# Two decoder layers on one core: the convolution's b gate by seven products instead of eight, its token sums in parts, and where its weights are summed and split

## The chip, the core and the metric

The kernel runs on one core of a Trainium2 chip. A core has five engines that run beside each other and wait for each other by semaphores: TensorE (PE in the profile; its weight loads are listed as PEld), VectorE (DVE), ScalarE (ACT), GpSimd (POOL) and SyncE (SP), which issues most of the DMAs. Operands lie in SBUF, 128 partitions wide; TensorE writes its sums to PSUM, eight banks of 128 x 512 numbers of 32 bits. The metric is the device time of one execution in microseconds, as the median of several runs; less is better. The profile is of one execution, taken by the hardware profiler.

## The reference

x has 512 tokens of 1024 features. Two layers: the first mixes tokens by attention with forget gates (16 heads), the second by a short gated convolution. Each is followed by an MLP with squared ReLU and by gated input embeddings, and all of them have norms before and behind. The part that the change is about is the second layer's mixer:

```python
def short_conv(h, w_in, conv_w, w_out):
    D = h.shape[-1]
    proj = h @ w_in
    b_gate = proj[..., :D]
    c_gate = proj[..., D:2 * D]
    u = proj[..., 2 * D:]
    z = c_gate * u
    zc = lax.conv_general_dilated(z, conv_w[:, None, :].astype(z.dtype), ...)
    return (b_gate * zc) @ w_out
```

and around it, for every layer,

```python
    x = x + rmsnorm(m, g[1])
    f = sq_relu_mlp(rmsnorm(x, g[2]), w_mlp_up[i], w_mlp_down[i])
    x = x + rmsnorm(f, g[3])
    gate = jax.nn.sigmoid(rmsnorm(x, g[4]) @ w_ple_gate[i])
    e = (p[i] @ w_ple_proj[i]) * gate
    x = x + rmsnorm(e, g[5])
```

## The kernel before

**Number format.** Every 32-bit operand of a matmul is split in a high part, rounded to the format that TensorE takes (a cast on ScalarE, L299), and a low part, the rest (a subtraction on VectorE or GpSimd, L300; the helper is `split`). A product is then three matmuls, high by high (L291), high by low and low by high (L292, L293; the helper is `mm3`). So each tile of weights, 128 x 512, costs a load of 256 KB, a cast and a subtraction before TensorE can use it. Casts and subtractions of tokens go by the same two lines.

**Weights.** `plan` lists all weight tiles in the order of use. `wide(key)` gives one of them and, first, has the next ones up to SOON = 8 beyond it loaded and split (`prepare`). Loads go through 14 raw buffers on SP's queue, split tiles through pages: there are 70 pages of 128 x 512, shared by nearly everything that lives in SBUF.

**Order.** The program is written in the order of the computation, and a scheduler puts the instructions of each engine in order from it, by its own estimate of times. Some work is put off until a number of columns was streamed (`put_off`), or until `need` asks for it: the transposes of normed tokens for example (`pre_norm`, `rate`).

**Seven products.** Where a matrix product is cut in 2 x 2 blocks, seven block products and some sums give what eight do. The down projections of the MLPs work so (`down`), and in the convolution the products for c and u. There, token halves L and R (256 tokens each) and halves of the input features cut the tokens in four parts, a11 to a22; halves of input and output features cut the weights in four quarters, b11 to b22. Sums of token parts are s1 to s4, sums of weight quarters t1 to t4. A unit, named 0, 2, 4 or 6 after the first of its two feature tiles, has seven products (`product`), each of two weight tiles and of 24 matmuls with 256 columns: four feature slices, three matmuls each, once for c and once for u. The results stay in PSUM until VectorE has combined them after COMBINE (L913; product 1 is copied by ScalarE first). `end` multiplies c by u (L925), and `finish` applies the three taps (L836 on ScalarE, L839 on VectorE), multiplies by b (L843) and splits the result, y.

**b.** b is a plain product, `times_b`: for each of eight feature tiles eight slices of three matmuls, with 512 columns; for unit 0 in two token halves (bL, bR). Its weights are 16 tiles, wcb.

**Order of the convolution.** CONV_ORDER lists, by unit, the products' numbers and the other steps: "embed" (a part of layer 1's embeddings that TensorE does here), "sums" (`token_sums`: all of s1 to s4 and their splits, L865 and L299/L300), b, and "end". Tokens 256 to 511 are first needed after "embed", where `need` asks for their transposes.

**Weight sums.** t1 to t4 are made in DRAM, before the convolution, by DMAs on GpSimd's queue: a copy of one quarter (L211) and a DMA that adds another (L213), 4 units by 4 sums, 32 steps of 512 KB. `sum_weights` issues the next step; it is called twice for each of four token blocks in attention's output product and in the gate products of layer 0, and 18 times in layer 0's MLP.

**Around it.** The gate stage (`ple`) of layer 0 goes through eight blocks of tokens and halves of features; for each 128 tokens `residual` adds its result to x and `pre_norm` scales x to the convolution's normed tokens, into pages of its own (n0b_h), which TensorE transposes later (n0b_p, L354). ScalarE copies the transposed tokens too (hp, L1229), for the token sums. After the convolution `mixer_out` multiplies y by w_o of the convolution (co) in the order of BLOCKS, eight slices k for each block. In attention, `bias` loads the mask and decay of a head by four DMAs on SP (L596) and masks them on GpSimd (L597); `scores` reads them on VectorE (L616).

Of the kernel before, what the change touches and what calls it, by code (L numbers as in the profile page):

```python
# [26 lines left out]
LAG = 2  # L27
AHEAD = 2
# [28 lines left out]

QUARTERS = ("b11", "b12", "b21", "b22")
SUMS_W = {"t1": ("b11", "b12"), "t3": ("b12", "b22"), "t2": ("t1", "b22"), "t4": ("t2", "b21")}
SUM_STEPS = (  # L60
    ("t1", "copy"), ("t3", "copy"), ("t1", "add"), ("t3", "add"), ("t2", "copy"), ("t2", "add"),
    ("t4", "copy"), ("t4", "add"),
)
# [26 lines left out]
def trunk(ctx: ExitStack, tc, g4T, x, xT, pT, g, g0T, wv, wqk, bf, wo, wcs, wcb, cw, wco, wup, wdn, wpp, wpg, out):  # L90
# [28 lines left out]
    g4_cols = []  # L119
# [78 lines left out]
    sums_w = {n: dram.tile([4, P, 2 * S], F32, tag=f"ws{n}", name=f"ws{n}") for n in SUMS_W}  # L198

    sum_steps = [(name, kind, i) for name, kind in SUM_STEPS for i in range(4)]  # L200

    def sum_weights():

        if not sum_steps:
            return
        of = lambda n, i: sums_w[n][i] if n in sums_w else wcs[QUARTERS.index(n), i]
        name, kind, i = sum_steps.pop(0)
        a, b = SUMS_W[name]
        with tc.issue_after(behind["add"].ins):
            if kind == "copy":  # L210
                nc.gpsimd.dma_start(sums_w[name][i], of(a, i))  # L211
            else:
                nc.gpsimd.dma_start(  # L213
                    sums_w[name][i], of(b, i), accum_op=ALU.add, max_dma_last_dim=2048
                )
# [12 lines left out]
    for l in range(2):  # L228
        if l == 0:
            for c, (_, width) in enumerate(V_CHUNKS):  # L230
                for k in range(KT * width // 512 if width < 272 else KT):
                    plan(("v", c, k), wv[c][k])
            for i in range(KT):
                for j in range(4):
                    plan(("qk", i, j), wqk[i, j])
            plan_embed(0)
            for k in range(KT):
                for n in range(2):
                    plan(("o", n, k), wo[n, k])
        else:  # L240
            for i0, i in CONV_ORDER:
                if i == "embed":
                    plan_embed(1)
                elif i == "bL" or i == "b":
                    for j in range(4):
                        plan(("b", i0, j), wcb[i0 // 2, j])
                elif i in PARTS:
                    n = PARTS[i][1]
                    src = sums_w[n] if n in sums_w else wcs[QUARTERS.index(n)]
                    for s in range(2):  # L250
                        plan(("sq", i0, s, n), src[i0 // 2][:, s * S : (s + 1) * S])
            for n in range(2):
                for k in range(KT):
                    plan(("co", n, k), wco[n, k])
# [88 lines left out]
    def scaled(t, n, xs, r, gB, name):  # L343
        h = page(f"{name}_h{t}_{n}")
# [4 lines left out]
        return h  # L349
# [30 lines left out]
    def pre_norm(t, xs, gB, hT, name, also=None):  # L380

        r = stats(t, xs, name)
        hs = [scaled(t, n, xs, r, gB, name) for n in range(2)]
# [56 lines left out]
    def mixer_out(kind, lhs, xs, gB, then, opened):  # L440


        mgs, sums = {}, {}
        for t, n in BLOCKS:
# [3 lines left out]
            ps = opened.pop((t, n)) if at else bank(f"{kind}{n}_{t}")  # L448
            for k in range(KT - 1 if at else 0, KT):
                mm3(ps, lhs(k, t), wide(kind, n, k, soon=soon(t, n)), k == 0, k == KT - 1)  # L450
            sums[t, n] = squares(ps, f"{kind}s{n}_{t}")
            mgs[t, n] = gained(ps, gB, n, f"{kind}m{n}_{t}")
            if (t, 1 - n) in mgs:
# [5 lines left out]
                if kind == "o":  # L459
                    sum_weights()  # L460
# [14 lines left out]
    def attention(hT, first_xT, g0_col, first_x, by_hand):  # L475
# [108 lines left out]
        def bias(h):  # L584
# [9 lines left out]
            for b, pr in enumerate(probs[h]):  # L594
                n = (b + 1) * P
                nc.sync.dma_start(pr, neg_c[b, h : h + 1, :n].partition_broadcast(P))  # L596
# [197 lines left out]
        for c in range(-SCORED, n_sc + LAG):  # L794
# [21 lines left out]
        return oT[0], banks_o  # L816

    def conv(hT, plain):
        taps = consts.tile([P, KT, 3], F32, tag="taps", name="taps")
        nc.sync.dma_start(taps, cw)  # L820
        ys = []
# [12 lines left out]
        def finish(i, z, y, b):  # L834
# [8 lines left out]
            nc.vector.tensor_tensor(out=a[:, :S], in0=b, in1=a[:, :S], op=ALU.mult)  # L843
# [9 lines left out]
        def token_sums():  # L853

            kept_at = {}
            for j in range(2):
                p = {(c, n): plain[2 * c + j, n][:, :S] for c in range(2) for n in range(2)}
                for name, a, b, op in (
                    ("s3", p[0, 0], p[1, 0], ALU.subtract), ("s1", p[1, 1], p[1, 0], ALU.subtract),
                    ("s2", p[0, 0], "s1", ALU.add), ("s4", "s2", p[0, 1], ALU.subtract),  # L860
                ):
                    t = page(f"{name}_{j}")
                    a, b = (kept_at[u, j] if isinstance(u, str) else u for u in (a, b))
                    kept_at[name, j] = t[:, :S]
                    nc.vector.tensor_tensor(out=t[:, :S], in0=a, in1=b, op=op)  # L865
            four = lambda u: u.rearrange("p (k c) -> p k c", k=4)
            two = lambda u: u[:, :S].rearrange("p (k c) -> p k c", k=2)
            for name in ("s3", "s1", "s2", "s4"):
                A[name] = [
                    Pair(page(f"{name}h{d}", F32R), page(f"{name}l{d}", F32R)).at(two)  # L870
                    for d in range(2)
                ]
                for d in range(2):
                    for j in range(2):
                        at = slice(j * P, (j + 1) * P)
                        split(
                            A[name][d].hi[:, :, at], A[name][d].lo[:, :, at],
                            four(kept_at[name, j])[:, 2 * d : 2 * d + 2, :],
                        )
# [37 lines left out]

        def end(i0):

            have = got.pop(i0)  # L920
            for e in range(2):
# [4 lines left out]
                y = Pair(page(f"yh{i}", F32R), page(f"yl{i}", F32R))  # L926
                finish(i, z, y, banks_b.pop((i0, e)))
                ys.append(y)

        need(0, 1)  # L930
        for i0, i in CONV_ORDER:
            if i == "embed":
                need(*range(NB))
            if i == "sums":
                token_sums()
# [146 lines left out]
    def ple(l, hT, xs, rs, gB, then):  # L1082
# [100 lines left out]
    for l in range(2):  # L1183
# [38 lines left out]
        if l == 0:  # L1222
# [8 lines left out]
            def then(t):  # L1231
                pre_norm(t, xs[t], g0, hT, "n0b", copied)
# [14 lines left out]
def layout(x, p, norm_g, w_attn_in, b_forget, w_attn_out, w_conv_in, conv_w, w_conv_out,  # L1247
# [26 lines left out]
    got["wcb"] = tiles(b.reshape(D, D), 2, 256)  # L1274
    cu = np.stack([c, u]).reshape(2, 2, 4, P, 4, 2, P)
    got["wcs"] = cu.transpose(1, 5, 4, 3, 0, 2, 6)[[0, 0, 1, 1], [0, 1, 0, 1]].reshape(4, 4, P, 2 * S)
# [26 lines left out]
```

## Time and profile before

| | us |
|---|---|
| median of 3 runs | 1215.29 |
| lowest and highest run | 1214.1, 1215.66 |
| the profiled execution | 1215.53 |
| its span, first to last instruction | 1213.8 |

The page of the profile lists each engine's busy time, then the chain of work that ended last: followed back from the last instruction, at each step to what released it. An engine with a large share of that chain sets the time. The page's groups join instructions of one line, engine and operation: "wl<-raw,wh ... x82 | 52.2, 683" is 82 instructions that write wl, together 52.2 us busy, 683 ns each. The rows of a timeline are: start, duration, engine, line, operation, tiles, count. Matmuls are pipelined, so one's duration overlaps the next one's; the distance of their starts is what one costs in a stream. A row of waits is: who waited for whom, total us, times, longest.

### The profile page before, as it was taken

The numbers are of one execution on the slowest core, as the hardware profiler recorded it, in microseconds if no ns is written. First come the engines' busy times: TensorE is split into PE (matmuls) and PEld (weight loads), VectorE is DVE, ScalarE is ACT, GpSimd is POOL, SyncE is SP. The second block draws the span as 40 slices with busy tenths as digits, with TensorE's granted clock in tenths as the row PEclk, the third lists the DMA queues.
The fourth block names the chain that finished last, engine by engine and source line by source line (L and its number), as shares of the span: only waits on it lengthen the run. The fifth ranks groups of instructions, "written<-read, shape, count | busy, mean of one in ns | idle before, by whom it ended". The sixth has DMA issues, their size and how long they took to land.

```text
span 1213.8 us, 18739 instructions
## 1 busy us (share of the span) xinstructions
PE 1203.1 (99%) x6176; PEld 1028.0 (85%) x6176; DVE 910.2 (75%) x1389; ACT 697.8 (57%) x1435; POOL 662.3 (55%) x691
## 2 busy tenths in 40 slices
PE   9999999999999999999999999999999999999997
PEld 8888888898888888888889999889888888888886
DVE  5668888575698779869867888665767886679963
ACT  7567888557634654465666555235755445535652
POOL 3057677167977798876221000017769777777420
PEclk9999999999999999999999999999999999999999
DMA  9564442673565566528357445732322442244501
GB/s 308 189 183 128 134 126 65 220 245 94 123 172 140 148 164 173 151 72 264 122 153 212 144 153 172 245 129 81 119 72 88 139 132 80 67 139 130 182 19 52
DMA packets 95377, 173.91 MB, mean 143 GB/s; under 512 B 11248, under 2 KB 18464, under 8 KB 95024
## 3 DMA queue, kind: packets, MB, share of 16 engines
q1 hardware_dynamic: 90272, 155.67, 40.1%
q0 software_dynamic: 4864, 16.78, 6.5%
q8 instruction: 49, 0.80, 0.3%
q14 instruction: 48, 0.39, 0.1%
q10 hardware_dynamic: 144, 0.26, 0.1%
HBM read 164.20 MB, written 25.25 MB: 156 GB/s over the span
## 4 chain that ended last, share of the span: by engine, by line
PE 96%; ACT 2%; DVE 1%; issue 1%; DVEq 0%; POOLq 0%; POOL 0%; ACTq 0%
PE up L293 10%; PE up L292 10%; PE up L291 10%; PE dn L293 9%; PE dn L291 8%; PE dn L292 8%; PE pg L293 2%; PE pg L291 2%; PE pg L292 2%; PE sq L293 2%; PE sq L292 2%; PE sq L291 2%; PE qk L291 2%; PE qk L292 2%; PE qk L293 2%; PE sc L610 1%
## 5 line engine op out<-in xcount | busy, mean ns | idle before, releaser
L300 DVE TENSOR_TENSOR wl<-raw,wh 128x512 fp32r<-128x512 f32 (+1 forms) x400 | 375.0, 980 | 41.7 <-ACT wh L299 37.6
L299 ACT CAST wh<-raw 128x512 fp32r<-128x512 f32 (+1 forms) x400 | 218.3, 619 | 12.4 <-DMA raw<-in_wv 3.7
L292 PE MATMUL up<-hTl,wh 128*128 128x512 f32 (+1 forms) x576 | 209.9, 366 | 0.0
L293 PE MATMUL up<-hTh,wl 128*128 128x512 f32 (+1 forms) x576 | 208.9, 365 | 0.0
L291 PE MATMUL up<-hTh,wh 128*128 128x512 f32 (+1 forms) x576 | 208.7, 366 | 0.0
L300 POOL TENSOR_TENSOR wl<-T,wh 128x512 fp32r<-128x512 f32 x112 | 157.2, 1434 | 25.4 <-ACT wh L299 24.1
L970 ACT ACTIVATE r<-up 128x512 f32<-128x512 f32 (+1 forms) x72 | 39.4, 548 | 197.3 <-PE up L293 197.3
L1018 DVE TENSOR_TENSOR acc<-dn,acc 128x512 f32<-128x512 f32 x168 | 107.8, 678 | 31.1 <-PE dn L293 31.0
L292 PEld LDWEIGHTS up<-hTl,wh 128*128 128x128 f32 x576 | 108.6, 189 | 17.5
L293 PEld LDWEIGHTS up<-hTh,wl 128*128 128x128 f32 x576 | 108.7, 189 | 17.4
L291 PEld LDWEIGHTS up<-hTh,wh 128*128 128x128 f32 x576 | 108.0, 189 | 17.6
L161 POOL TENSOR_TENSOR T<-raw,raw 128x512 f32<-128x512 f32 x56 | 85.8, 1544 | 59.7 <-DMA raw<-in_wdn 28.2
L161 POOL TENSOR_TENSOR T<-raw,T 128x512 f32<-128x512 f32 x56 | 89.0, 1589 | 2.2
L321 POOL TENSOR_SCALAR cor_r_v<-cos,cos 128x1 f32<-128x1 f32 x4 | 1.2, 302 | 155.5 <-ACT junk L337 155.5
L299 ACT CAST wh<-T 128x512 fp32r<-128x512 f32 x112 | 61.5, 617 | 10.4 <-POOL T L161 10.4
L300 DVE TENSOR_TENSOR A12l<-q,A12h 128x512 fp32r<-128x512 f32 x28 | 30.1, 1074 | 42.8 <-ACT A12h L299 42.8
L300 DVE TENSOR_TENSOR A11l<-q,A11h 128x256 fp32r<-128x256 f32 x28 | 26.1, 933 | 35.9 <-ACT A11h L299 35.9
L1025 POOL TENSOR_TENSOR acc<-acc,acc 128x512 f32<-128x512 f32 x28 | 47.1, 1714 | 10.0 <-DVE acc L1018 10.0
L299 ACT CAST S1h<-s 128x512 fp32r<-128x512 f32 x28 | 17.4, 621 | 60.8 <-POOL s L985 60.8
L293 PE MATMUL pg<-wh,hTl 128*128 128x512 f32 (+1 forms) x136 | 51.8, 381 | 0.0
L291 PE MATMUL pg<-wh,hTh 128*128 128x512 f32 (+1 forms) x136 | 51.6, 379 | 0.0
L292 PE MATMUL pg<-wl,hTh 128*128 128x512 f32 (+1 forms) x136 | 51.4, 378 | 0.0
(327 smaller groups left out, 3302.2 us busy)
## 6 DMA issues: line engine op xcount, KB each, us to landing
raw<-in_wup SPq DMA_DIRECT2D x128, 256.0 KB, 2.9
raw<-in_wdn SPq DMA_DIRECT2D x128, 256.0 KB, 2.8
wst<-in_wcs POOLq DMA_DIRECT2D x24, 512.0 KB, 6.7
raw<-in_wqk SPq DMA_DIRECT2D x32, 256.0 KB, 4.8
raw<-in_wpg SPq DMA_DIRECT2D x32, 256.0 KB, 3.2
raw<-wst SPq DMA_DIRECT2D x32, 256.0 KB, 3.6
raw<-in_wcs SPq DMA_DIRECT2D x24, 256.0 KB, 4.0
g<-in_g SPq DMA_DIRECT2D x18, 256.0 KB, 5.4
```

Source lines behind the costliest of these rows:

```text
L161: nc.gpsimd.tensor_tensor(out=B[name, p], in0=B[a, p], in1=B[b, p], op=ALU.subtract)
L291: nc.tensor.matmul(ps, a.hi, b.hi, start=start, stop=False)
L292: nc.tensor.matmul(ps, a.hi, b.lo, start=False, stop=False)
L293: nc.tensor.matmul(ps, a.lo, b.hi, start=False, stop=stop)
L299: nc.scalar.copy(hi, src)
L300: eng.tensor_tensor(out=lo, in0=src, in1=hi.bitcast(F32), op=ALU.subtract)
L321: nc.gpsimd.tensor_scalar(out=v, in0=parts[0], scalar1=parts[1], scalar2=EPS, op0=ALU.add, op1=ALU.add)
L610: nc.tensor.matmul(ps[:, :nm], at[:, b * P : n], to[:, :nm], start=s == 0, stop=s == 1)
L970: nc.scalar.activation(r[:, :n], ps[:, :n], AF.Relu)
L1018: nc.vector.tensor_tensor(out=a, in0=banks[s], in1=a, op=ALU.add)
L1025: nc.gpsimd.tensor_tensor(out=a, in0=a, in1=acc[i, s][:, :S], op=ALU.add)
```

## The change

- **b by seven products.** Two more units, "b0" and "b4", give b for feature tiles 0 to 3 and 4 to 7, by the same `product`: what were c and u are now two pairs of b's feature tiles. The four quarters of the weights, and t1 to t4, have six units instead of four; `times_b` isn't called any more. `end` of a unit of c and u stops after the taps, and `end` of b0 or b4 weighs four results, in token halves (`weigh`), and splits them.
- **Token sums in parts.** `token_sums` makes s1 and s2 (splitting s2), then s3, then the split of s1, then s4, as steps of their own between the products of units 0 and 2, whose order is interleaved.
- **Normed tokens.** `pre_norm` writes them to the pages that held the gated embeddings' products of the same tokens (`freed`), not to new ones.
- **Splits in the gate stage.** Before the gate products' last two blocks in layer 0 four weight tiles more are prepared, and eight more at the start of the convolution.
- **Weight sums.** The copies (24 now) go to SP's queue, two after each `bias` of heads 2 to 15; the additions (24) stay on GpSimd's, one at each block of attention's output product.
- **Output product of the convolution.** Slices k are taken in the order 0, 1, 2, 3, 4, 6, 5, 7, and the first four of them for two blocks ahead of the rest.

```diff
+CO_ORDER = (0, 1, 2, 3, 4, 6, 5, 7)
+CO_FIRST = 4
+SPLIT_AT = {"s1s2": "s2", "s3": "s3", "s1": "s1", "s4": "s4"}
+SUMS_OF = {"s1s2": ("s1", "s2"), "s3": ("s3",), "s1": (), "s4": ("s4",)}
+UNITS = (0, 2, "b0", 4, 6, "b4")
 CONV_ORDER = (
-    [(0, i) for i in (1, 2, "bL", "embed", 4, "sums", "bR")] + [(2, 1), (2, 2)]
-    + [(0, i) for i in (7, 5, 6, 3, "end")] + [(2, i) for i in (6, 7, 5, 4, 3, "b", "end")]
-    + [(i0, i) for i0 in (4, 6) for i in (1, 6, 7, 5, 2, 4, 3, "b", "end")]
+    [(0, 1), (0, 2), (2, 1), (2, 2), (0, "s1s2"), (0, "embed"), (0, 4), (2, 4), (0, "s3")]+ [(0, 6), (0, "s1"), (2, 6), (0, 7), (0, "s4"),  (0, 5), (2, 7), (0, 3), (2, 5), (0, "end"), (2, 3)]
+    + [("b0", 1), ("b0", 6), (2, "end")] + [("b0", i) for i in (7, 5, 3, 4, 2)]
+    + [(4, 1), ("b0", "end")] + [(4, i) for i in (6, 7, 5, 2, 4, 3)] + [(6, 1), (6, 6), (4, "end")]
+    + [(6, i) for i in (7, 5, 2, 4, 3)] + [("b4", 1), ("b4", 6), (6, "end")]
+    + [("b4", i) for i in (7, 5, 3, 4, 2, "end")]
 )
...
+    def copy_sums():
+        if sum_copies:
+            n, u = sum_copies.pop(0)
+            with tc.issue_after(behind["bias"].ins):
+                nc.sync.dma_start(of(n, u), of(SUMS_W[n][0], u))
...
+        if kind == "co":
+            for t, n in BLOCKS[:2]:
+                ps = bank(f"{kind}{n}_{t}")
+                for k in CO_ORDER[:CO_FIRST]:
+                    mm3(ps, lhs(k, t), wide(kind, n, k, soon=SOON), k == 0, False)
+                opened[t, n] = ps, CO_ORDER[:CO_FIRST]
...
                 if kind == "o":
                     sum_weights()
                 then(t)
-                if kind == "o":
-                    sum_weights()
...
                     bias(h)
+                    copy_sums()
+                    copy_sums()
...
+        def weigh(a, y, b):
+            for at, m in b:
+                nc.vector.tensor_tensor(out=a[:, at], in0=m, in1=a[:, at], op=ALU.mult)
             split(y.hi[:, :S], y.lo[:, :S], a[:, :S])
...
+            if i0 in ("b0", "b4"):
+                b = got.pop(i0)
+                for e in range(2):
+                    for i1 in ((0, 2) if i0 == "b0" else (4, 6)):
+                        y = Pair(page(f"yh{i1 + e}", F32R), page(f"yl{i1 + e}", F32R))
+                        weigh(halfway.pop(i1 + e), y, [
+                            (at, b[f"c{h + 1}{e + 1}"][:, R if i1 in (2, 6) else L])
+                            for h, at in enumerate((L, R))
+                        ])
+                        ys[i1 + e] = y
+                return
...
         need(0, 1)
+        prepare(begun[0] + 8)
...
+            if l == 0 and (t, n) == (2, 0):
+                prepare(begun[0] + 4)
...
-                residual(t, *([d.pop((t, i)) for i in range(2)] for d in (mgs, sums)), xs[t],
-                         f"er{l}")
+                freed[t], q = ([d.pop((t, i)) for i in range(2)] for d in (mgs, sums))
+                residual(t, freed[t], q, xs[t], f"er{l}")
...
-                pre_norm(t, xs[t], g0, hT, "n0b", copied)
+                pre_norm(t, xs[t], freed[t], g0, hT, "n0b", copied)
...
+    bq = b.reshape(2, 4, P, 2, 2, 2, P).transpose(0, 5, 3, 2, 4, 1, 6)
     cu = np.stack([c, u]).reshape(2, 2, 4, P, 4, 2, P)
+    cu = cu.transpose(1, 5, 4, 3, 0, 2, 6)
+    units = [cu[:, :, :2], bq[:, :, :1], cu[:, :, 2:], bq[:, :, 1:]]
+    got["wcs"] = np.concatenate(units, axis=2).reshape(4, 6, P, 2 * S)
```

More of the change, by code (lines that the diff above doesn't have):

```diff
@@ L197, in trunk @@
     behind, ahead = {}, {}
-    sums_w = {n: dram.tile([4, P, 2 * S], F32, tag=f"ws{n}", name=f"ws{n}") for n in SUMS_W}
-    sum_steps = [(name, kind, i) for name, kind in SUM_STEPS for i in range(4)]
-    def sum_weights():
[L204 to L212, printed above, removed]
+    sums_w = {
+        n: dram.tile([len(UNITS), P, 2 * S], F32, tag=f"ws{n}", name=f"ws{n}") for n in SUMS_W
+    }
+    of = lambda n, u: (sums_w[n] if n in sums_w else wcs[QUARTERS.index(n)])[UNITS.index(u)]
+    sum_copies = [(n, u) for n in ("t1", "t3", "t2", "t4") for u in UNITS]
+    sum_steps = list(sum_copies)
+    def copy_sums():
[3 more added lines that the diff above has]
+                nc.sync.dma_start(of(n, u), of(SUMS_W[n][0], u))
+    def sum_weights():
+        if sum_steps:
+            n, u = sum_steps.pop(0)
+            with tc.issue_after(behind["add"].ins):
                 nc.gpsimd.dma_start(
-                    sums_w[name][i], of(b, i), accum_op=ALU.add, max_dma_last_dim=2048
+                    of(n, u), of(SUMS_W[n][1], u), accum_op=ALU.add, max_dma_last_dim=2048
                 )
@@ L348, in scaled @@
         )
-        return h
     def turned(t, n, h, name):
@@ L447, in mixer_out @@
             at = (t, n) in opened
-            ps = opened.pop((t, n)) if at else bank(f"{kind}{n}_{t}")
-            for k in range(KT - 1 if at else 0, KT):
-                mm3(ps, lhs(k, t), wide(kind, n, k, soon=soon(t, n)), k == 0, k == KT - 1)
+            ps, done = opened.pop((t, n)) if at else (bank(f"{kind}{n}_{t}"), ())
+            todo = [k for k in (CO_ORDER if kind == "co" else range(KT)) if k not in done]
+            for k in todo:
+                mm3(
+                    ps, lhs(k, t), wide(kind, n, k, soon=soon(t, n)),
+                    not done and k == todo[0], k == todo[-1],
+                )
             sums[t, n] = squares(ps, f"{kind}s{n}_{t}")
@@ L595, in bias @@
                 n = (b + 1) * P
-                nc.sync.dma_start(pr, neg_c[b, h : h + 1, :n].partition_broadcast(P))
+                behind["bias"] = nc.sync.dma_start(
+                    pr, neg_c[b, h : h + 1, :n].partition_broadcast(P)
+                )
                 nc.gpsimd.affine_select(
@@ L813, in attention @@
                     bias(h)
+                    copy_sums()
+                    copy_sums()
         for _ in main:
             pass
-        return oT[0], banks_o
+        return oT[0], {at: (ps, range(KT - 1)) for at, ps in banks_o.items()}
     def conv(hT, plain):
@@ L820, in conv @@
         nc.sync.dma_start(taps, cw)
-        ys = []
+        ys = {}
         def times_b(i0, lo, hi):
@@ L851, in conv @@
         }
[L853 to L865, printed above, removed]
+        kept_at = {}
@@ L866, in token_sums @@
+        def token_sums(wanted):
             four = lambda u: u.rearrange("p (k c) -> p k c", k=4)
             two = lambda u: u[:, :S].rearrange("p (k c) -> p k c", k=2)
[L868 to L872, printed above, removed]
-                for d in range(2):
[L874 to L879, printed above, removed]
+            for name in SUMS_OF[wanted]:
+                for j in range(2):
+                    p = {
+                        f"p{c}{n}": plain[2 * c + j, n][:, :S] for c in range(2) for n in range(2)
+                    }
+                    t = page(f"{name}_{j}")
+                    a, b = (p.get(u) or kept_at[u, j] for u in SUM_OF[name][:2])
+                    kept_at[name, j] = t[:, :S]
+                    nc.vector.tensor_tensor(out=t[:, :S], in0=a, in1=b, op=SUM_OF[name][2])
+            name = SPLIT_AT[wanted]
+            A[name] = [
+                Pair(page(f"{name}h{d}", F32R), page(f"{name}l{d}", F32R)).at(two)
+                for d in range(2)
+            ]
+            for j in range(2):
+                for d in range(2):
+                    at = slice(j * P, (j + 1) * P)
+                    split(
+                        A[name][d].hi[:, :, at], A[name][d].lo[:, :, at],
+                        four(kept_at[name, j])[:, 2 * d : 2 * d + 2, :],
+                    )
```

45 lines of the change are left out of this document (23 added, 22 removed).

## The prediction

> **What bounds the kernel now.** I read the page's list of engines first, then the chain that ended last, then TensorE's own waits, and then three stretches around the convolution.
>
> ```profile
> span 1213.8 us, 18739 instructions
> PE 1203.1 (99%) x6176; PEld 1028.0 (85%) x6176; DVE 910.2 (75%) x1389; ACT 697.8 (57%) x1435; POOL 662.3 (55%) x691
> PE 96%; ACT 2%; DVE 1%; issue 1%; DVEq 0%; POOLq 0%; POOL 0%; ACTq 0%
> ```
> ```profile
> PE idle L1174 <- DVE warm L1159: 1.5, 1, 1.5
> PE ps_o L651 <- ACT ph L299: 0.8, 2, 0.5
> PE dn L293 <- DVE A12l L300: 0.3, 1, 0.3
> ```
> ```profile
> 600.00:644.00 44.00, 44.00 (x211) 36.58 (x210) 29.19 (x45) 28.24 (x63) 11.98 (x24) 1.00 0.52 136
> 644.00:776.20 132.20, 132.20 (x954) 125.55 (x953) 110.93 (x192) 68.58 (x136) 2.35 (x5) 1.00 0.57 181
> 776.20:810.00 33.80, 33.80 (x155) 28.10 (x154) 13.11 (x20) 9.51 (x24) 3.27 (x7) 1.00 0.45 156
> ```
>
> TensorE is busy for 99% of the span and carries 96% of the chain. Its largest wait inside the work is 0.8 us. The columns of the stretches are: length, then busy time of PE, weight loads, VectorE, ScalarE and GpSimd, then granted clock, DMA share and GB/s. The gate stage of layer 0 (600 to 644), the convolution (644 to 776.2) and the start of its output product have no gap on TensorE at clock 1.00. So only less TensorE work can shorten these 210 us, and a change there can lose by opening a gap. VectorE is the next engine: 110.93 of 132.20 us, 84%, in the convolution, but 66% in the gate stage and 39% after 776.2.
>
> **TensorE's saving.** A busy time of pipelined matmuls overlaps its neighbours, so I take the distance from one start to the next.
>
> ```profile
> 703.05 0.40 PE L291 MATMUL b<-hTh,wh 128*128 128x512 f32 x1
> 713.28 0.39 PE L291 MATMUL b<-hTh,wh 128*128 128x512 f32 x1
> ...
> 650.11 0.28 PE L293 MATMUL b<-hTh,wl 128*128 128x256 f32 x1
> 655.39 0.29 PE L293 MATMUL b<-hTh,wl 128*128 128x256 f32 x1
> 655.52 1.91 PE L354 MATMUL n0b_p<-ident,n0b_h 128*128 128x128 f32 x16
> 657.18 0.48 PE L291 MATMUL ppa<-wh,wh 128*128 128x512 f32 x1
> ```
> ```profile
> L291 PE MATMUL sq<-hTh,wh 128*128 128x256 f32 x96 | 27.0, 283 | 0.0
> L291 PE MATMUL b<-hTh,wh 128*128 128x512 f32 x48 | 18.7, 390 | 0.0
> L291 PE MATMUL b<-hTh,wh 128*128 128x256 f32 x32 | 8.7, 283 | 0.0
> ```
>
> 45 steps of 512 columns take 10.23 us, 0.2273 each; 44 steps of 256 columns take 5.28 us, 0.120 each. Two halves cost 0.240, 5.6% more than a whole. Each of the three lines (L291 to L293) has 48 wide and 32 narrow b matmuls, so b costs now 144 x 0.2273 + 96 x 0.120 = 44.25 us. A check of the method: 28 products of 24 narrow matmuls (80.64), b (44.25), 24 wide ones of the embedding (5.46) and 16 transposes (655.52 to 657.18, 1.66) make 132.0, and the stretch has 132.2. There is no hidden stall.
>
> After the change b is two units of seven products, 14 x 24 = 336 narrow matmuls: 40.32 us. **The saving is 3.93 us**, far less than the eighth that is left out of the multiplications, because narrow matmuls are dearer. The stage would need 128.3 us. [...]
>
> **VectorE's added work.** Its cadence is read the same way.
>
> ```profile
> 763.56 2.48 DVE L300 TENSOR_TENSOR wl<-raw,wh 128x512 fp32r<-128x512 f32 x4
> 765.97 0.68 DVE L913 TENSOR_TENSOR U<-U,sq 128x512 f32<-128x512 f32 x1
> ...
> 743.75 1.53 DVE L839 SCALAR_TENSOR_TENSOR za<-cp,taps,za 128x511 f32<-128x511 f32 x2
> 745.38 0.69 DVE L843 TENSOR_TENSOR za<-b,za 128x512 f32<-128x512 f32 x1
> ...
> 666.99 1.28 DVE L865 TENSOR_TENSOR s<-hp,hp 128x512 f32<-128x512 f32 x2
> 668.31 0.69 DVE L865 TENSOR_TENSOR s<-hp,s 128x512 f32<-128x512 f32 x1
> ...
> 672.31 1.43 DVE L300 TENSOR_TENSOR s3l<-s,s3h 128x256 fp32r<-128x256 f32 x4
> 673.65 1.43 DVE L300 TENSOR_TENSOR s1l<-s,s1h 128x256 fp32r<-128x256 f32 x4
> ```
>
> So a weight tile's low part, or a combination of two products, costs 0.60 us, a tap 0.8, a token sum 0.66, a 256-column operation 0.34. The weights go from 56 + 16 tiles to 84: 12 more, 7.2 us. Two units more make 14 combinations (L913), 8.4 us. The weighing of z by b (L843) becomes 16 halves instead of 8 wholes, about 5.4 against 5.2. Together **15.8 us more**: 126.7 of VectorE in 128.3 of TensorE, if nothing leaves the stage. Two things leave it. The four tiles split in the gate stage take 2.4 us there, where 14.8 us are free. The eight tiles of the output weights' second half, which that stage split early, are first needed after two blocks of 24 wide matmuls (10.9 us) of that product, and may go there: 4.8 us. That leaves 119.5 of 128.3, 93%. ScalarE takes 12 casts and 2 copies more and stays near 60%.
>
> Where is it tight? Two places, counted from 644.
>
> ```profile
> L1229 ACT COPY hp<-n0b_p x8: 568/587/632, 631.6 to 660.6; 128x512 f32<-128x512 f32 x8
> ```
>
> The last transposed token page is copied at 661.2, and the transposes keep their place: four products come before them (11.5 us) as now. Behind them come the embedding (5.5) and the two products with t4 (5.8), so the first that needs s2 starts near 668.6. Four token sums (2.64) and four narrow splits (1.36) end near 665.5: in time by 3 us. Splitting the token work thus removes the block of 10.7 us (666.99 on) that stood in one piece. The next eight products take 23.0 us, and VectorE has for them s3, s1 and s4 (6.7), 12 combinations (7.2), 16 tiles (9.6) and the taps and gate products of unit 0 (4.6): 28.1. The 5.1 missing are 8.5 tiles of lead. The lead is 8 tiles, and 4.6 of the 28.1 are the taps, which TensorE doesn't need before b0 ends. If they are queued behind the weights, TensorE waits for nothing.
>
> ```profile
> 776.94 0.69 DVE L843 TENSOR_TENSOR za<-b,za 128x512 f32<-128x512 f32 x1
> 778.32 0.69 DVE L300 TENSOR_TENSOR yl<-za,yh 128x512 fp32r<-128x512 f32 x1 [0.69 <-ACT yh L299]
> ```
>
> The other place is the hand-over. Now the last y is ready at 779.0, covered by the seven other k of the first output block. After the change four y wait for the last product: a combination of 0.60, then as here 2.06 from the start of the weighing to the end of the low part, so the first y is there some 3 us after the product, and each of the others 1.3 later (two halves and one low part), the last at 7. Two blocks' first four k, 24 x 0.2273 = 5.5 us, stand between, and the four k after them start at 5.5, 6.1, 6.8 and 7.5. It fits by 0.5 us at the last; without that cover it would cost 3 to 7. For both places I take a wait as in the one row where VectorE held up TensorE outside attention, 0.3 us: 0.6 together.
>
> **Pages and loads.** The normed tokens take the gate products' pages, which are read just before them on VectorE: nothing is added, and eight pages come free for the four earlier tiles.
>
> ```profile
> 635.38 2.50 DVE L300 TENSOR_TENSOR wl<-raw,wh 128x512 fp32r<-128x512 f32 x4 [0.58 <-ACT wh L299]
> SPq L148 <- DMA wst<-in_wcs: 5.5, 1, 5.5
> ```
>
> Eight tiles of the convolution were ready before 644 (the last four here). If no page is free for more, this part costs nothing against before, but gains nothing. The weight sums' adds end earlier (24 steps against 32, of which two, not six, fall in the gate stage), so the one wait of SP for them goes; TensorE never felt it. Worth: 0.
>
> **Copies on SP in attention.** 24 copies of 512 KB go from GpSimd's queue after attention to SP's between the bias loads, two behind each.
>
> ```profile
> 84.00:190.00 106.00, 104.81 (x557) 88.22 (x556) 90.79 (x253) 85.78 (x205) 78.25 (x128) 1.00 0.46 132
> q0 software_dynamic: 254, 4.19, 34.4%
> wst<-in_wcs POOLq DMA_DIRECT2D x8, 512.0 KB, 6.7
> ```
> ```profile
> 108.55 0.80 SPq L596 DMA_DIRECT2D prr<-neg_c  x2
> 115.45 0.54 POOL L597 TENSOR_SCALAR_AFFINE_SELECT prr<-prr 128x128 f32<-128x128 f32 x2
> 125.49 0.27 DVE L616 CUSTOM_DVE_ANT_0 prr<-sc,prr 128x128 f32<-128x128 f32 x1
> ```
>
> In 228 to 264 eight such copies took 34.4% of the DMA engines: 1.55 us each. 24 make 37 us, over 106 us of attention: the share goes from 0.46 to 0.81. A bias that was masked at 115.45 is used at 125.49, with 9.5 us to spare; the four copies of a pair of heads take 6.2 of them. So 0, with the loads of w_o behind them as far ahead. The removed issues give GpSimd time that no one waits for: 0.
>
> **Sum.** On the profiled execution (1215.53 us, 1.7 of it outside the span): 1215.53 - 3.93 + 0.6 = 1212.2. It stands 0.24 above the median, so the forecast for the median is **1212.0**.
>
> **The rivals.** (a) *VectorE late for some products*, 23%. The taps stand ahead of the weights, or pages hold the lead at four tiles: 5.1 - 2.4 = 2.7 us are missing in the eight products after 668.6, and about 1 at the hand-over. With the saving that gives 1215. For it: the 28.1 against 23.0. Against: the lead. (b) *VectorE becomes the bound of the stage*, 14%, the slower side. Its densest stretch so far is this:
>
> ```profile
> 664.00:700.00 36.00, 36.00 (x302) 36.00 (x302) 31.06 (x60) 17.96 (x41) 0.00 (x0) 1.00 0.50 163
> ```
>
> 86%, with waits for casts and products between. If 88% is all that it can hold, 119.5 becomes 135.8 us, 3.6 over before: 1218.9. It decides from a share of 119.5 / 132.2 = 90% downwards. Against it: here VectorE ran ahead of need and could idle. (c) *Biases late*, 6%: if the copies ran one after another at the landing time of 6.7, four take 27 us, 17 more than the slack; even a tenth of that for six pairs is 10 us, 1222. The 1.55 speaks against. [...] No run here shows a bias behind a copy in one queue. (d) *The saving isn't there*, because the narrow matmuls with other weights run slower or lose their order, 5%: 1215.
>
> **How the numbers follow.** The forecast has 52%. This kernel's measurement can tell about 0.2% (2.4 us) from no change, so faster means under 1212.9: the forecast, 52%. (a) and (d) make 28% for the same, (b) and (c) 20% for slower. The range reaches from no wait at all, 1211.4, less the 1.2 us by which the lowest run lies under the median, 1210.2, up to (b), 1219.0; it leaves out (c) and the edges.
>
> **What would show it.** Right: 336 more sq matmuls 0.12 apart and no b; the stage near 128.5 us; VectorE at 92% or more in it; no PE wait over 0.5 us there. Wrong: PE waits for wl, s or yl between 668 and 692 (a), such waits throughout, in units 4 to b4 as well (b), waits for prr or prl in attention (c), a spacing over 0.12 (d). I would be most wrong if VectorE's queue holds the taps of a unit ahead of the weights of the next.

## The result and the profile after

| | before | after |
|---|---|---|
| median, us (lowest to highest) | 1215.3 (1214.1 to 1215.66) | 1225.02 (1222.45 to 1227.0) |
| ratio, with its 95% interval | | 1.008 [1.0067, 1.0094] |
| the profiled execution, us | 1215.53 | 1226.5 |

The changed kernel is slower by 9.7 us (0.8%; the interval of the ratio lies above 1), where 3.3 less were forecast, and it lies outside the range. The page of the changed kernel, its head and its chain:

```profile
span 1224.8 us, 19020 instructions
PE 1203.1 (98%) x6272; PEld 1034.1 (84%) x6272; DVE 918.9 (75%) x1423; ACT 704.5 (58%) x1449; POOL 668.4 (55%) x683
...
PE 89%; DMA 4%; POOL 2%; issue 2%; DVE 1%; ACT 1%; SPq 0%; POOLq 0%; DVEq 0%
```

TensorE's busy time is the same, but its share of the chain fell from 96% to 89%, and DMA and GpSimd stand in it. To see where the time came in, I take the first start of three groups of matmuls, by tile: up (the first MLP), sq (the first product of the convolution) and co (its output product). The stretch before "to" is the first start. Before:

```profile
L291 PE MATMUL up<-hTh,wh x576: 277/389/389, 256.2 to 1131.5; 128*128 128x512 f32 x148, 128*128 128x256 f32 x44
...
L291 PE MATMUL sq<-hTh,wh x96: 277/283/283, 644.0 to 761.9; 128*128 128x256 f32 x96
...
L291 PE MATMUL co<-wh,yh x64: 389/389/476, 776.1 to 820.7; 128*128 128x512 f32 x64
```

After:

```profile
L302 PE MATMUL up<-hTh,wh x576: 278/389/389, 271.5 to 1142.2; 128*128 128x512 f32 x148, 128*128 128x256 f32 x44
...
L302 PE MATMUL sq<-hTh,wh x96: 277/283/283, 658.9 to 763.6; 128*128 128x256 f32 x96
...
L302 PE MATMUL co<-wh,yh x64: 389/389/476, 787.0 to 831.7; 128*128 128x512 f32 x64
```

Up to the first MLP 15.3 us are lost (256.2 to 271.5). From there to the convolution 0.4 come back. The convolution itself, sq to co, shrank from 132.1 to 128.1: 4.0 us, as forecast. The sum is 10.9, and the span grew by 11.0. So the change did what it was for, and lost nearly four times as much in attention, before its own stage began. TensorE's waits of the changed kernel say at whom:

```profile
PE ps_o L671 <- POOL ph L656: 9.7, 4, 3.1
PE pT L649 <- POOL prl L642: 2.3, 1, 2.3
```

These five waits for GpSimd are all in attention. Before, there was one:

```profile
PE ps_o L651 <- POOL ph L636: 0.2, 1, 0.2
```

Stretches (length, busy times, clock, DMA share, GB/s) of attention before and, in the second fence, after, with two of the five waits and the 4 us behind each:

```profile
70.00:222.00 152.00, 150.07 (x796) 126.28 (x795) 126.78 (x352) 122.81 (x293) 100.99 (x164) 1.00 0.42 123
```
```profile
70.00:222.00 152.00, 139.71 (x722) 118.13 (x721) 114.24 (x326) 112.28 (x270) 97.65 (x156) 0.97 0.61 191
...
106.00:110.00 4.00, 0.88 (x4) 0.46 (x3) 1.87 (x8) 2.50 (x7) 2.38 (x6) 0.96 0.89 323
110.00:114.00 4.00, 4.00 (x16) 3.23 (x16) 0.00 (x0) 0.20 (x1) 3.39 (x3) 0.62 0.45 129
150.00:154.00 4.00, 2.01 (x12) 1.78 (x13) 1.05 (x5) 1.86 (x5) 3.98 (x7) 1.00 0.75 265
154.00:158.00 4.00, 4.00 (x25) 3.53 (x25) 3.09 (x11) 2.89 (x10) 3.50 (x5) 1.00 1.00 103
```

TensorE was idle for 12.3 us of this stretch instead of 1.9: 10.4 of the 15.3. The rest is the clock: behind three of the five waits it fell (0.04 and 0.38 of 4 us at 106 to 114, 1.7 us), behind two it didn't (150 to 158 is one of them, at 1.00). Three times 1.7 is 5.1, and 10.4 + 5.1 = 15.5.

**Why GpSimd is late.** GpSimd's waits in 84 to 200 before, then after:

```profile
POOL prr L622 <- DVE rs L621: 13.9, 10, 2.6
POOL prl L622 <- DVE rs L621: 8.2, 11, 1.5
POOL pr L622 <- DVE rs L621: 3.2, 6, 1.0
POOL prr L597 <- DMA prr<-neg_c: 2.1, 2, 1.4
POOL prl L597 <- DMA prl<-neg_c: 1.2, 3, 0.5
```
```profile
POOL prr L617 <- DMA prr<-neg_c: 21.0, 16, 3.2
POOL prl L617 <- DMA prl<-neg_c: 7.9, 6, 2.2
POOL pr L617 <- DMA pr<-neg_c: 4.2, 6, 0.9
POOL prr L642 <- DVE rs L641: 2.0, 2, 1.6
```

Before, GpSimd waited 25.3 us for the sums of the softmax (rs), that is, for its input: it ran ahead. For biases it waited 3.6 us. After, it waits 33.1 us for biases and hardly for rs: it no longer runs ahead, and what stands behind a waiting mask in its queue comes late. One of the five waits in GpSimd's timeline (in brackets: idle before, and for whom):

```profile
188.23 0.29 POOL L617 TENSOR_SCALAR_AFFINE_SELECT prr<-prr 128x128 f32<-128x128 f32 x1 [1.25 <-DMA prr<-neg_c]
190.45 0.84 POOL L617 TENSOR_SCALAR_AFFINE_SELECT prr<-prr 128x128 f32<-128x128 f32 x1 [1.93 <-DMA prr<-neg_c]
191.28 2.19 POOL L642 TENSOR_SCALAR prr<-prr,rs 128x384 f32<-128x384 f32 x1
193.43 0.29 POOL L617 TENSOR_SCALAR_AFFINE_SELECT prl<-prl 128x128 f32<-128x128 f32 x1
193.66 0.20 POOL L656 MEMSET ph<- 128x128 f32 x1
```

Two masks of heads to come wait 3.2 us for their biases. Behind them stand a normalization, another mask and a memset of 0.2 us (ph), and for that memset TensorE waits 2.26 us, until 193.92. The biases come late because of the copies. SP's issues in the changed kernel:

```profile
111.62 0.38 SPq L614 DMA_DIRECT2D prl<-neg_c  x1
112.15 2.01 SPq L218 DMA_DIRECT2D wst<-in_wcs  x2
114.20 1.49 SPq L614 DMA_DIRECT2D pr<-neg_c  x1
...
118.75 3.53 SPq L218 DMA_DIRECT2D wst<-in_wcs  x2
```

and the transfers of 84 to 200, size and median from issue to landing, before and after:

```profile
prl<-neg_c SPq DMA_DIRECT2D x12, 256.0 KB, 6.7
prr<-neg_c SPq DMA_DIRECT2D x12, 192.0 KB, 6.4
...
prr<-neg_c SPq DMA_DIRECT2D x12, 64.0 KB, 4.4
```
```profile
wst<-in_wcs SPq DMA_DIRECT2D x20, 512.0 KB, 11.0
...
prl<-neg_c SPq DMA_DIRECT2D x12, 256.0 KB, 9.0
prr<-neg_c SPq DMA_DIRECT2D x12, 192.0 KB, 8.3
```

The second head's biases are issued behind the first head's copies, and each bias takes some 2 us more to land (1.7 to 2.8 by the medians of the four sizes).

### The profile page after: what moved, and what is told of

The parts are those of the page before. It is cut to its first block, busy times and chain, and to the rows that moved or that the text cites. A ratio compares the mean times of both kernels' runs of the same rounds, so it can differ in the third digit from the quotient of the medians.

```text
span 1224.8 us, 19020 instructions
## 1 busy us (share of the span) xinstructions
PE 1203.1 (98%) x6272; PEld 1034.1 (84%) x6272; DVE 918.9 (75%) x1423; ACT 704.5 (58%) x1449; POOL 668.4 (55%) x683
## 4 chain that ended last, share of the span: by engine, by line
PE 89%; DMA 4%; POOL 2%; issue 2%; DVE 1%; ACT 1%; SPq 0%; POOLq 0%; DVEq 0%
PE up L302 10%; PE up L304 10%; PE up L303 10%; PE dn L304 8%; PE dn L302 8%; PE dn L303 8%; PE pg L304 2%; PE pg L302 2%; PE pg L303 2%; PE sq L304 2%; PE sq L303 2%; PE sq L302 2%; PE o L303 1%; PE o L302 1%; PE o L304 1%
## 5 line engine op out<-in xcount | busy, mean ns | idle before, releaser
L311 DVE TENSOR_TENSOR wl<-raw,wh 128x512 fp32r<-128x512 f32 (+1 forms) x412 | 381.9, 970 | 38.7 <-ACT wh L310 38.4
L310 ACT CAST wh<-raw 128x512 fp32r<-128x512 f32 (+1 forms) x412 | 224.3, 618 | 7.3 <-DMA raw<-in_wv 3.9
L311 POOL TENSOR_TENSOR wl<-T,wh 128x512 fp32r<-128x512 f32 x112 | 156.8, 1430 | 24.3 <-ACT wh L310 20.1
L302 PE MATMUL qk<-hTh,wh 128*128 128x512 f32 x128 | 52.2, 408 | 0.0
```

The costliest lines, as they stand in the source:

```text
L302: nc.tensor.matmul(ps, a.hi, b.hi, start=start, stop=False)
L310: nc.scalar.copy(hi, src)
L311: eng.tensor_tensor(out=lo, in0=src, in1=hi.bitcast(F32), op=ALU.subtract)
```

## The experiments

The theory: the copies in attention cost the time, by late biases. Its rivals: something else of the change costs it (the order, pages or splits), and the convolution's saving is worth less than it seems; and, among the ways in which copies could hurt, the queue they share, their number, their bytes at that moment, or who waits. "Up" is the first start of the tile up; the kernel before had medians of 1215.5 to 1215.7 in these runs.

| run | median, us (range) | ratio to before | up |
|---|---|---|---|
| e1 copies after attention | 1211.77 (1211.32 to 1213.39) | 0.9971 [0.996, 0.9982] | 257.1 |
| e2 before, with copies | 1227.23 (1226.74 to 1227.86) | 1.0096 [1.0083, 1.011] | 268.9 |
| e6 four behind a pair | 1215.23 (1211.93 to 1219.76) | 0.9993 [0.9979, 1.0007] | 260.9 |
| e4 ScalarE's queue | 1228.08 (1227.34 to 1229.01) | 1.0103 [1.009, 1.0117] | 273.7 |
| e7 e1 + quarter copies | 1212.51 (1211.11 to 1214.01) | 0.9975 [0.9964, 0.9986] | |
| e15 e1 + half copies | 1212.41 (1211.8 to 1214.4) | 0.9977 [0.9968, 0.9987] | |
| e3 masks later | 1248.7 (1247.13 to 1249.49) | 1.0271 [1.0257, 1.0285] | 293.7 |
| e8 e3's order on e1 | 1247.43 (1246.14 to 1248.71) | 1.0261 [1.0241, 1.0282] | |
| e9 masks wait for nothing | 1217.86 (1214.91 to 1220.72) | 1.002 [1.0011, 1.0029] | 264.8 |
| e13 the same, in place | 1217.92 (1215.15 to 1218.77) | 1.0013 [1.0004, 1.0023] | 263.3 |
| e14 e13's edit on e1 | 1211.36 (1210.62 to 1211.93) | 0.9965 [0.9952, 0.9978] | 255.8 |
| e5 copies on GpSimd's queue | 1225.76 (1224.99 to 1226.17) | 1.0082 [1.0067, 1.0097] | 256.8 |
| e10 no early splits | 1212.88 (1211.86 to 1213.63) | 0.9978 [0.9969, 0.9988] | |
| e11 no slices first | 1211.32 (1210.57 to 1212.45) | 0.9967 [0.9954, 0.998] | |
| e12 token sums in one | 1211.82 (1211.01 to 1212.88) | 0.9971 [0.9961, 0.9982] | |

**e1: the copies alone undone.** They stay on SP's queue, but go out after attention, one at each step of the weight sums; the additions start four steps later.

```diff
-                    copy_sums()
-                    copy_sums()
...
     def sum_weights():
-        if sum_steps:
+        copy_sums()
+        slots.append(0)
+        if sum_steps and len(slots) > 4:
```

> The changed kernel, but the 24 copies of weight quarters go on SP's queue behind attention, at the places where a weight sum's step stands (attention's output product, MLP and gate stage of layer 0), each four places ahead of its addition. Theory Q (in attention the copies stand ahead of the bias loads in SP's queue; GpSimd's masks wait for the biases, and what is queued behind them, normalizations and memsets, reaches TensorE late): first up matmul back from 271.5 to about 256.2, no TensorE wait for GpSimd over 0.5 us, and with the convolution 4.0 us shorter a time of 1211.3 (1210.5 to 1212.5). Theory O (another part of the change delays attention, for example a new order of instructions): still about 1225.

**e2: the copies alone done.** The kernel before, with its own 16 copies moved to SP's queue behind the biases of heads 2 to 9; GpSimd keeps the 16 additions, and all else is as it was.

```diff
                     bias(h)
+                    copy_sums()
+                    copy_sums()
```

> The kernel before with one part of the change alone: its 16 copies on SP's queue, two behind each of the biases of heads 2 to 9; the rest as before. Theory Q: two thirds of the copies give about two thirds of the 15.3 us lost in attention, 10 us: 1225 (1221 to 1228), with TensorE waiting for GpSimd's memsets of ph. Theory O: 1215.3, the time of before.

e1 takes the loss away: 1211.8, 13.2 us under the changed kernel, and faster than both kernels. Up starts 0.9 us later than before (257.1 against 256.2), and one wait of TensorE for GpSimd, 1.6 us, is left; the expectation had none over 0.5. e2 shows the loss without the rest of the change: 11.7 us over the kernel before, by 16 copies, more than the two thirds (10 us) that were expected of them. GpSimd's waits of e1 in 84 to 200 are again near those of before:

```profile
POOL prr L648 <- DVE rs L647: 13.6, 9, 2.6
...
POOL prl L623 <- DMA prl<-neg_c: 2.5, 4, 1.0
POOL prr L623 <- DMA prr<-neg_c: 2.4, 3, 1.4
```

So the loss comes with the copies, and without them hardly any of it is left; and the convolution's saving is real: e1 stands 3.8 us under before.

**e6, e4: is it the queue?** e6 puts the same copies behind the second head of a pair only; e4 leaves their places and issues them on ScalarE's queue.

```diff
-                    copy_sums()
-                    copy_sums()
+                    for _ in range(4 * (h % 2)):
+                        copy_sums()
```

> The changed kernel with the copies still on SP's queue in attention, but four behind the bias of each second head, none between the two heads' biases; TensorE's order is that of the changed kernel. Theory Q (a copy hurts the biases behind it in the same queue): only the next pair's biases, some 9 us later, stand behind copies, so they land in 6.7 us and the time is 1211 to 1214. Theory B (bandwidth taken away in attention as a whole): as the changed kernel, 1222 to 1227.

```diff
-            with tc.issue_after(behind["bias"].ins):
-                nc.sync.dma_start(of(n, u), of(SUMS_W[n][0], u))
+            with tc.issue_after(behind["exp"].ins):
+                nc.scalar.dma_start(of(n, u), of(SUMS_W[n][0], u))
```

> The changed kernel with the copies at the same places in attention, issued by ScalarE on its own DMA queue. Theory Q, first link (the same queue): biases land in 6.6 us as before (median), GpSimd's wait for them falls by more than half, the time to 1212 to 1219; ScalarE pays some 0.4 us for each issue, 10 us in all, of which a part may show. Theory B (bandwidth: 12 MB more in 110 us slow every transfer, whatever its queue): biases at 7.5 us or more, 1223 to 1228. [...]

e6 recovers 9.8 of the 13.2 us with the same bytes on the same queue, with a wide range of times: what matters is which biases a copy meets. Its median lies 1.2 us above what theory Q allowed and far under theory B; its biases land in 6.7 to 7.4 us (the medians of the four sizes), the smallest still late (6.7 against 4.4 before). In e4 no bias stands behind a copy in its queue, and it is as bad as the changed kernel. There the biases still land late (the row for those of 256 KB; 6.7 before), GpSimd still waits 27.1 us for them, and the issuing engine adds waits of its own:

```profile
prl<-neg_c SPq DMA_DIRECT2D x11, 256.0 KB, 8.4
```
```profile
PE ps_o L673 <- ACT ph L310: 4.5, 4, 2.6
PE ps_o L673 <- POOL ph L658: 3.5, 2, 3.4
```

So in e4 a queue of its own didn't protect a bias: 8.4 us to land for those of 256 KB, 6.7 before. SP also takes longer to issue the biases: 29.3 us in the changed kernel for the 48 of them in 84 to 200, 22.3 before (but 29.3 in e15 below too, where little is lost). How much of e4's loss is ScalarE's part was not taken apart.

**e7, e15: number or bytes?** To e1, 24 more copies into a spare tensor, at the places where the changed kernel has its copies: of 128 KB in e7 (its diff is shown), of 256 KB in e15 (64 rows for 32).

```diff
+                nc.sync.dma_start(spare[len(part_copies)], of(SUMS_W[n][0], u)[:32])
...
                     bias(h)
+                    for _ in range(2):
+                        part_copy()
```

> The kernel of e1 with 24 copies of 128 KB into a spare place of DRAM added in attention, at the places where the changed kernel has its copies of 512 KB: as many DMAs on SP's queue, a quarter of the bytes. If the bytes count (theory Q or B): a quarter of the 13 us between e1 and the changed kernel, 1215 (1212.5 to 1217). If the number of DMAs or SP's time for issuing them counts: 1221 or more.

> As e7, with 24 extra copies of 256 KB instead of 128 KB in attention. 128 KB cost 0.7 us, 512 KB 13. If the cost begins where the delay of the biases uses up the slack of GpSimd's queue (a threshold): 1213 to 1216, well below half of 13. If bytes cost in proportion beyond a small one: 1217 to 1219.

Each costs 0.6 to 0.7 us, inside the intervals; e7 lies at the low end of what its first expectation allowed, e15 just under its first. The number of DMAs isn't it, and the loss isn't in proportion to the bytes either: half of them cost next to nothing, the whole 13 us. GpSimd's waits for biases in 84 to 200 put these runs in order: 3.6 us before, 6.7 in e1, 7.7 in e7, 15.7 in e15, 20.1 in e6 (3.5 us over e1), 22.7 in e2 (11.7 over before), 33.1 in the changed kernel (13.2 over e1). e4 stands outside this order, with 27.1 us and a loss of 16.3, in which ScalarE has its part. My reading, which no run tests by itself: waiting for a bias is free as long as it replaces waiting for rs, of which there were 25.3 us; as it comes in single pieces of up to 3 us, the loss begins somewhat under that.

**e3, e8, e9, e13, e14: who waits?** If only the masks in GpSimd's queue carry the lateness on, masks that don't hold anything up should cure it. e3 puts each mask behind the normalization of the scores before; e8 does that to e1.

```diff
+                if at + 2 < n_sc:
+                    for e in range(2):
+                        mask((at + 2) // 8 * 2 + e, (at + 2) % 8 // 2)
```

> The changed kernel with its copies in attention, but each mask (affine_select) is put in GpSimd's order behind the normalization of the scores before, one step ahead of the scores that need it, not right behind the bias loads. Theory Q with GpSimd's order as its link: biases land as late as in the changed kernel (median near 7.8 us against 6.6), but GpSimd waits for them by less than 15 us (78 in the changed kernel, over the whole kernel), TensorE's waits for GpSimd fall from 12 to below 4, and the time to 1211 to 1216. If the late biases hurt by VectorE's own wait for them, or by something else: 1223 to 1227.

> The kernel of e1 (no copies in attention) with the masks' place of e3: what that order costs by itself. If e3's 1248.7 came from the order alone, about 1236 to 1248 here, and e3 says nothing of the copies; if the order is free, about 1212.

A miss: the new order alone costs 36 us (e8 against e1), with or without copies. In e3 GpSimd waits for no bias any more, but for rs up to 12 us at a time, and TensorE has new waits, the largest for VectorE's pl (6.8 us in four). So e3 says nothing of the copies. Instead, in e9, e13 and e14, the mask works on a spare tile, so that it waits for no bias; the causal mask is left out of the scores in these three. In e9 all 64 masks ran in the first 25 us, which takes their time out of attention as well; e13 keeps them between the normalizations (the diff's last line), and e14 is the same without copies in attention.

```diff
-                    out=pr[:, b * P : n], in_=pr[:, b * P : n], compare_op=ALU.is_ge,
+                    out=scrap[:, b * P : n], in_=scrap[:, b * P : n], compare_op=ALU.is_ge,
...
+                with tc.issue_after(behind["norm"].ins) if "norm" in behind else nullcontext():
```

> The changed kernel, copies in attention as they are, but GpSimd's masks work on a spare tile instead of the loaded biases (the causal mask is left out of the scores; as many instructions of the same size in the same order): only their wait for the DMAs is gone. Theory G (biases land 1.2 us later, but what costs the time is that GpSimd, 74% busy and in order, stands before the masks and brings the normalizations late): 1210 to 1213, GpSimd's wait for biases gone, no TensorE wait for GpSimd over 1.6 us. If the late biases or the copies' traffic hurt in another way (VectorE's own wait for biases, late weight loads): 1219 to 1227.

> As e9 (the changed kernel, copies in attention, masks on a spare tile, the causal mask left out), but the masks stay between the normalizations in GpSimd's order; in e9 all 64 ran in the first 25 us, so that GpSimd also had 18 us less to do in attention. TensorE's and VectorE's orders are those of the changed kernel. If the wait of GpSimd before the masks makes the loss, and not its load: as e9, 1216 to 1219, so 7 of 13 us are GpSimd's wait and 6 are VectorE's own wait for biases and late loads. If it was the load: 1221 to 1226.

> The control of e13: the same masks on the spare tile (causal mask left out), but the copies behind attention as in e1. What the copies cost when GpSimd doesn't wait for biases is e13 less this. Both theories: near e1, 1210.5 to 1212.5.

With masks that wait, the copies cost 13.2 us (1225.0 against 1211.8); with masks that don't, 6.6 (1217.92 against 1211.36). So about half of the loss goes away when GpSimd doesn't wait. What is left is a bias that is late for its own use on VectorE (e13's rows, by VectorE's and TensorE's waits):

```profile
DVE prr L640 <- DMA prr<-neg_c: 7.0, 5, 4.2
```
```profile
PE pT L655 <- DVE nmx L640: 3.6, 3, 2.8
```

e14 has neither of these waits, and TensorE is idle in 70 to 222 for 1.7 us there, in e13 for 6.1. In the changed kernel itself VectorE waits for a bias only 0.2 us, as the mask is there first; so the two halves are what is won by freeing the masks and what stays, not two waits that stand beside each other.

**e5: could GpSimd have kept the copies?** e1 with the copies on GpSimd's queue, as before.

```diff
-                nc.sync.dma_start(of(n, u), of(SUMS_W[n][0], u))
+                nc.gpsimd.dma_start(of(n, u), of(SUMS_W[n][0], u))
```

> As e1, but the copies behind attention are issued by GpSimd, as in the kernel before. TensorE waits for nothing in these stages in either, so 1211.4 (1210.5 to 1212.5), the same as e1; if GpSimd's 24 issues of 0.55 us delay the sums for the MLP's weights, up to 1214.

A miss: 14 us over e1, in another place. Up starts at 256.8, but the convolution 12 us later than in e1, at 656.2. Its 24 copies (0.54 us each on GpSimd) and 24 additions (0.93) take 35 us of GpSimd there; the 32 steps of the kernel before took 23. TensorE's waits in e5 are in the MLP (7.6 us idle from 257 to 656 with a clock of 0.99; none in e1, at 1.00):

```profile
PE dn L308 <- DVE S1l L315: 5.6, 4, 2.0
```

That the 12 us more of GpSimd delay these sums is argued from the waits, not shown by a run of its own. But in this place b's two units can't have their copies from GpSimd for nothing.

**e10, e11, e12: three parts of the change undone on e1.** e10 drops the two early `prepare` calls, e11 sets CO_FIRST to 0, e12 makes all token sums at one place, behind "embed" (of CONV_ORDER's line only the part that changes is shown).

```diff
-        prepare(begun[0] + 8)
...
-CO_FIRST = 4
+CO_FIRST = 0
...
-(0, "embed"), (0, 4), (2, 4), (0, "s3")]+ [(0, 6), (0, "s1"), (2, 6), (0, 7), (0, "s4"),  (0, 5),
+(0, "embed"), (0, "s3"), (0, "s1"), (0, "s4"), (0, 4), (2, 4)] + [(0, 6), (2, 6), (0, 7), (0, 5),
```

> The kernel of e1 without the two early preparations (four weight tiles in the gate stage, eight at the convolution's start). If these carry VectorE through the tight products, as my ledger of 28.1 us of work in 23.0 has it: TensorE waits for wl, s or yl in the convolution, 1 to 3 us, 1213 to 1215. If VectorE has room without them: 1211.8, and a convolution of 128.1 us.

> The kernel of e1 with no slices of the output product taken ahead (CO_FIRST 0): block (0, 0) starts slice 4 right after its first four, 2.7 us after the last product of b4 instead of 5.5. By my working of the hand-over, where the first y stands 3 us and the last 7 us after that product, TensorE waits 0.3 to 2.8 us: 1212 to 1214.5. If VectorE is ahead there: 1211.8.

> The kernel of e1 with all token sums right behind s1 and s2, ahead of the two products with t4, instead of between the products. 10.7 us of VectorE in one piece from 661 on would end near 672, and the first product with s2 starts near 668: if the order is kept, a wait of 2 to 4 us, 1214 to 1216. If the scheduler or VectorE's lead absorbs it: 1211.8.

None costs over 1.1 us, and the intervals of all three overlap e1's. From sq to co they take 128.8, 128.1 and 128.2 us, against 128.1 in e1. e10 has the one wait in the convolution that its expectation named, for s3l, but of 0.3 us. e11 doesn't test what it was meant to: its first 61 matmuls of the output product come in the same order as in e1, by their tiles, so the scheduler takes the slices ahead by itself, and what they are worth stays open. In e12 VectorE does the sums in one piece, from 659.6 to 670.6, and s2 is split before the products need it.

## Why the prediction was wrong, step by step

**TensorE's saving: right.** 3.93 us forecast, 4.0 measured (132.1 to 128.1), and 128.1 again in e1.

**VectorE's added work: right, and with more room than I took.** It is busy for 116.9 of the 128.1 us in the changed kernel, where I had 119.5 of 128.3, and the convolution shows no wait for VectorE, where I had set 0.6. The densest stretch of it in the changed kernel, then nearly the whole in e1:

```profile
700.00:735.00 35.00, 35.00 (x294) 35.00 (x293) 33.24 (x60) 17.10 (x32) 0.00 (x0) 1.00 0.62 202
```
```profile
645.00:772.00 127.00, 127.00 (x1041) 126.05 (x1040) 116.07 (x208) 71.00 (x143) 6.31 (x6) 1.00 0.56 179
```

VectorE works 91% of the convolution, 95% over 35 us, and TensorE never stops. So rival (b), by which 88% is all that VectorE can hold, falls. Rival (a) needed late products between 668 and 692; none was late, and even the token sums in one piece (e12) are in time. The hand-over came out at no wait by luck. I had the four y ready 3 to 7 us after the start of the output product, covered by 5.5 us of slices. In e1, where that product starts at 772.34, they are ready from 778.8 to 780.6, at 6.5 to 8.3 us:

```profile
778.14 2.50 DVE L315 TENSOR_TENSOR yl<-za,yh 128x512 fp32r<-128x512 f32 x4 [0.43 <-ACT yh L314]
```

Nothing waits because 27 matmuls (6.1 us), not 24, run slice by slice ahead, and behind them the order mixes slices. That is the scheduler's doing; the changed kernel and e11 have the same order.

**Pages, splits and additions: 0, right** as far as the runs show: the splits within 1.1 us (e10); pages and additions have no run of their own, but e1, with both, is 0.2 us under the forecast.

**Copies on SP in attention: 0. This step failed.** It failed in three places, each of which the profile before gave reason to doubt.

- *The wrong end of the slack.* I read it from the mask (115.45) to the use on VectorE (125.49): 9.5 us. But the mask is the first to need the bias. Two issues stood at 108.55, landing takes 4.4 us for prr's 64 KB and 6.4 for its 192 KB, and the masks ran at 115.45: by these medians the slack was 0.5 to 2.5 us.
- *The queue behind the wait.* A mask that waits holds up GpSimd's normalizations and memsets of other heads, 33.1 us in all, more than the 25.3 us that GpSimd had waited for its input. I didn't name what stands behind it. By e13 and e14, half of the loss goes when masks don't wait.
- *The price.* I took 1.55 us a copy, a share of 16 DMA engines. The rows of the changed kernel show a copy beside the biases for longer: it lands in 11.0 us, a bias some 2 us later than before, and SP's issue of the next head's biases moves behind the copies.

To it comes the clock, which no term of the sum had: 5 us of the 15.3.

Rival (c), 1222 us with 6%, is what happened, in nearly its size (1225.0). Its condition, copies that run one after another at the landing time of 6.7, no run shows. What the runs show is that the place of the copies matters (e6, 9.8 of the 13.2 us), and that another queue didn't help (e4, 1228.1). I weighed (c) by a row for copies that ran where no bias was being loaded, and that row couldn't speak for or against it. That its size came near is luck: the tenth of the delay that (c) let through had no row behind it. The rest of my sum held: e1, which has everything but this step, was measured at 1211.8, against the forecast of 1212.0.

One row I read too high: TensorE's 0.8 us before is the total of two waits, the longest 0.5. Nothing in the sum hangs on it.

## What to carry to other kernels

The slack of a transfer ends at its first consumer (here a mask at 115.45, not VectorE at 125.49), and the price of being late includes what is queued behind that consumer on its engine (about half of the 13.2 us here, by e13 and e14); so look for the engine's waits for its other inputs, which are the slack that may be used up (25.3 us of them here). Don't move large transfers beside small ones that land just in time without a test, and don't count on another queue to protect them (8.4 us for a bias in e4, 6.7 before); in this kernel the same copies cost nothing that shows once attention is over, and that version (e1) keeps the convolution's gain and beats both kernels. A gain worked out well in one stage says nothing of the stage from which its helpers were paid.

## What the hardware did that I had not expected

The clock after a wait. TensorE's rows of the changed kernel behind the wait that ends at 193.92:

```profile
193.92 0.39 PE L671 MATMUL ps_o<-ph,v 128*128 128x256 f32 x1 [2.26 <-POOL ph L656]
...
196.83 0.63 PE L303 MATMUL qk<-hTl,wh 128*128 128x512 f32 x1
197.25 0.63 PE L304 MATMUL qk<-hTh,wl 128*128 128x512 f32 x1
197.68 0.63 PE L671 MATMUL ps_o<-ph,v 128*128 128x512 f32 x1
```

Matmuls of 512 columns start 0.42 us apart, where 0.227 is usual; the granted clock was 0.62 in 194 to 198 and 0.95 in 198 to 202. So this wait of 2.26 us cost TensorE some 1.7 us more, and two others did the same (0.82 and 0.75 in 90 to 98, 0.96 and 0.62 in 106 to 114).

The length of a wait doesn't tell whether the drop comes. Three of the five waits had it: 90.34 to 92.60 (2.26 us), 106.51 to 109.63 (3.12) and 191.66 to 193.92 (2.26). Two didn't, with a clock of 1.00 in 150 to 158 and in 170 to 178: 149.95 to 151.99 (2.04) and 170.66 to 172.93 (2.27). By the spacing of the matmuls, full speed is back at 96.0, 113.1 and 198.4, 3.4 to 4.5 us after the wait. Behind the last of the three waits four matmuls still come at the usual spacing, and the slow ones begin at about 194.9. What decides between the three and the two wasn't shown: these are five waits of one trace, and no run was made to test it.

The other surprise is the step between 256 KB and 512 KB: 24 copies of the one cost 0.6 us, of the other 13.2, with the biases of 256 KB landing at 8.0 against 9.0 us.
